# A hybrid Fourier and mLSTM block on one core: the transfers that build block sums issued at other units of the weight stream, and a last block product in fresh banks

## The chip, the cores and the metric

The kernel runs on one core of a Trainium2 chip. The metric is device time in microseconds (us). The kernel before takes 780.82 us (median of 3 runs, 779.57 to 783.08). The profiled execution took 779.69 us, with a span of 777.9 us between its first and its last instruction.

The core's engines run their own instruction streams: TensorE multiplies (PE in the profile; PEld is its weight load), VectorE (DVE), ScalarE (ACT) and GpSimd (POOL) work on tiles, and SyncE (SP) issues transfers. POOL issues some transfers too. Every stream is in order: an instruction that waits holds up what stands behind it.

## The reference

The block has 512 positions (S) and 1024 channels (D), batch 1, one layer:

```python
h = rmsnorm(x, norm_w)
x_f, z_f, x_m, z_m, o_m, g_logits = split(h @ w_in)     # 1024, 1024, 2048, 2048, 2048, 2048 columns
y_a = (fourier_mix(x_f) * silu(z_f)) @ w_fourier        # Re of a 2-D DFT over positions and group channels
x_c = silu(centred_dwconv(x_m))                         # q, k from x_c and v from x_m, block-diagonal
h_cell = mlstm_fwd(q, k, v, gates) + mlstm_bwd(...)     # 4 heads of 512, chunks of 128 positions
h_cell = rmsnorm_per_head(h_cell * sigmoid(o_m)) * hnorm_w
y_b = ((h_cell + skip_w * x_c) * silu(z_m)) @ w_mlstm
g_a, g_b = split(sigmoid(g_logits))
x = x + (g_a * y_a + g_b * y_b) @ w_out
return rmsnorm(x, final_norm_w)
```

All of it is float32.

## The kernel before

**Products.** A float32 product is done as three products of rounded halves: high by high, low by high and high by low (`mm3`, lines 95 to 98). The weights come in units of 128 x 1024 numbers (512 KB), which `plan` lists in their order of use. For each unit SP issues a transfer into one of three buffers `raw` (lines 130 and 133); ScalarE copies the high half (`whi` or `gwh`, `hi_of`, line 86) and VectorE subtracts it for the low half (`wlo` or `gwl`, `lo_of`, line 89). `unit` hands out the next split unit and keeps two items ahead (four once the pool "gw" is open, which is from the stage of the groups on). A transfer can start when the unit that was in its buffer is split.

**Stages.** The units 0 to 16 serve the first projections, 17 to 47 the four heads with their gates, 48 to 63 `w_mlstm`. From unit 64 on come the groups: 16 column groups of `w_in` (the gates of the merge, x_f and z_f) are multiplied by the Strassen-Winograd scheme, seven products of half-size blocks for eight (`group`, with `seventh` and `fourth` for the two products that are put off into the next group). A product there is 12 matmuls of 256 columns, a unit holds two blocks. Between them stands the DFT. Then come eight units of `w_fourier`, then the out-projection by the same scheme in wide form (`wide_product`, seven products on the halves of the 512 rows), the residual, and the final RMSNorm.

**Block sums.** The scheme needs four sums S1 to S4 of blocks of the weights, for four stacks of four groups and for the out-projection (NB = 5 stacks, 20 sums of 1 MB). They are made from DRAM to DRAM: job i (`sum_job`, lines 155 to 162) has SP copy a block into the tile of sum i (line 158), and POOL add another block to sum i-1 with an accumulating transfer (line 162), which has to wait for its copy. In the profile and the program order the tiles are called `sum_76` to `sum_95`: four for each stack, stack 0 (`sum_76` to `sum_79`) being read first, from unit 64 on, and stack 4 (`sum_92` to `sum_95`) by the out-projection. Before, `unit` issues a job each time the next unit to be split is 11, 14, 17 and so on (lines 164 to 168), 21 jobs up to unit 71.

**Heads.** At the end of each head, when its output has been multiplied by the o-gate, the rows are normalised: POOL computes the reciprocal root of four row blocks (`rr`, lines 627 and 628), VectorE scales by it (line 629) and TensorE transposes (line 639). POOL also applies the triangular masks (`wf_...`, AFFINE_SELECT, lines 504 and 507).

**The end.** The out-projection accumulates in X, Z and Y, each two banks of 512 columns, one for each of the two row blocks of 128 (t) in a half of the rows. When a product is done, VectorE adds or subtracts its bank to or from the residual tile `yb` (`add`, line 984). When the last contribution to a tile is in, `part` takes its sum of squares on ScalarE (line 942) and collects it on POOL, and `finish` takes the reciprocal root on POOL (line 953), scales both halves (lines 957, 959, 961) and writes out (line 962). The row blocks 2 and 3 finish before 0 and 1. For row block 1, the last one, the final norm's weight `fn` is multiplied in before (line 949), so that only a scaling by the root is left. The last product is added on top of X, whose bank serves both halves (`0:256`, `256:512`) of row block 1.

**Order.** The program is written in the order of the stages, and a scheduler with a simulated timeline orders the instructions of each engine; `pin` keeps the weight transfers and the copies of the sums in program order on SP. A job moved to another unit therefore also moves what stands around it on SP, POOL and, by way of the weights, on ScalarE.

Of the kernel before, what the change touches and what calls it, by code (L numbers as in the profile page):

```python
# [11 lines left out]
ALU = mybir.AluOpType  # L12
AX = mybir.AxisListType

S = 512
# [4 lines left out]
NRAW = 3  # L20
NG = 16
NB = 5
JOB_AT, JOB_STEP = 11, 3
NWARM = 13
XO = (4, 5, 6, 7, 8, 9, 10, 11, 12, 13, 14, 15, 0, 1, 2, 3)
NU0 = 3
# [13 lines left out]
def hybrid_block(ctx: ExitStack, tc, xT, xn, units, blocks, vecs, gates, gbias, consts, dft, fnw, out):  # L40
    nc = tc.nc
    te, ve, se, gp = nc.tensor, nc.vector, nc.scalar, nc.gpsimd
# [35 lines left out]
    def bank(tag, cols=512, rows=P):  # L78
        count[0] += 1
        return ps.tile([rows, cols], F32, tag=tag, name=f"{tag}_{count[0]}", bufs=4)  # L80
# [41 lines left out]
    state = {"raw": 0, "split": 0, "job": 0}  # L122
# [40 lines left out]

    def unit():
        i = state["split"]
        if i >= JOB_AT and (i - JOB_AT) % JOB_STEP == 0 and state["job"] <= 4 * NB:
            sum_job(state["job"])
            state["job"] += 1
        while len(items) < (4 if "gw" in pools else 2) and state["split"] < nplan:
            prepare()  # L170
        return items.pop(0)
# [63 lines left out]
    def wview(name):  # L235
        return vc[:, name : name + 64].rearrange("p (i d) -> p i d", i=16)
# [18 lines left out]
    ve.tensor_tensor(out=prod, in0=wkr, in1=wview(V_WQ).unsqueeze(2).to_broadcast([P, 16, 4, 4]), op=ALU.mult)  # L255
    ve.tensor_reduce(out=m4, in_=prod, axis=AX.X, op=ALU.add)
    ve.tensor_scalar(out=m4, in0=m4, scalar1=float(512.0 ** -0.5), scalar2=None, op0=ALU.mult)
# [10 lines left out]
    def fold_gates():  # L268
        folded.append(True)
        folds = [tl("sa0", [P, 2, 16, 16]), tl("sb0", [P, 1, 16, 16])]  # L270
        for j, off in enumerate((V_WQ, V_WK, V_WV)):
            dst = folds[j // 2][:, j % 2]
            for half in range(2):
# [3 lines left out]
                ve.tensor_tensor(out=g, in0=g, in1=w, op=ALU.mult)  # L277
                ve.tensor_reduce(out=dst[:, hs, :], in_=g, axis=AX.X, op=ALU.add)
        f = folds[0]
# [83 lines left out]
    for n, (kind, i) in enumerate([("z", 0)] + [("x", i) for i in XO]):  # L363
# [4 lines left out]
        acc = proj(hooks)  # L368
# [76 lines left out]
    half = tl("half", [P, 2, 2])  # L445
# [8 lines left out]
    for h in range(NH):  # L454
# [21 lines left out]
        for d in range(4):  # L476
            acc = bank("wk")
# [70 lines left out]
        for b in range(4):  # L548
            n = (b + 1) * P
# [4 lines left out]
        for acc, first, rest, off in ((sf, 0, (1, 2, 3), P), (sb_, 3, (2, 1, 0), 0)):  # L554
            for b in rest:
                n = (b + 1) * P
                rng = slice(n - P, S) if off else slice(0, n)
                wr = slice(n, 640) if off else slice(0, n)
                if b == rest[0]:
                    full = slice(P, 640) if off else slice(0, S)  # L560
# [31 lines left out]
        for b in range(4):  # L592
            n = (b + 1) * P
# [80 lines left out]
    for q in range(2):  # L674
        accs = [bank("acc") for _ in range(4)]
# [34 lines left out]
    def seventh():  # L710
        X, out1, p5, func, then = prev[0]
        product(X, t_hi, t_lo, 2, False)
        o = out1[:, 256:512]
        ve.scalar_tensor_tensor(out=o, in0=X, scalar=-1.0, in1=p5, op0=ALU.mult, op1=ALU.subtract)
        if func:
            se.activation(o, o, func)

    def fourth():
        X, out1, p5, func, then = prev.pop(0)
        product(X, t_hi, t_lo, 3, False)  # L720
# [4 lines left out]
    def group(out0, out1, func=None, then=None):  # L725
# [4 lines left out]
        if prev:  # L730
            seventh()
        Z = bank("wk")[:, 0:256]
        product(Z, t_hi, t_lo, 0, True)
        se.activation(p5, Z, AF.Copy)
        Y = bank("wk")[:, 0:256]
        product(Y, b_hi, b_lo, 1, True)
        ve.tensor_tensor(out=out0[:, 0:256], in0=Y, in1=p1, op=ALU.add)
        product(X, t_hi, t_lo, 1, False)
        se.activation(u2, X, AF.Copy)
        if prev:  # L740
            fourth()
        product(Z, b_hi, b_lo, 2, False)
        ve.tensor_tensor(out=out0[:, 256:512], in0=Z, in1=u2, op=ALU.add)
        if func:
# [151 lines left out]
    mb, mt = {}, {}  # L896
    for j in range(8):
        ga = gates_a[j]
        wh, wl = unit()
        acc = bank("acc")  # L900
# [16 lines left out]
        else:  # L917
            k = j - 4
# [19 lines left out]
    def part(t, half, cs):  # L938
        y = res[t, half][:, cs]
        sq = t2k()[:, 0 : cs.stop - cs.start]  # L940
        ss = tl("fss", [P, 1], bufs=4)
        se.activation(sq, y, AF.Square, scale=1.0 / 32.0, accum_out=ss)
        if t not in rows:
            rows[t] = tl("rr", [P, 1], bufs=4)
            gp.tensor_scalar(out=rows[t], in0=ss, scalar1=EPS, scalar2=None, op0=ALU.add)
        else:
            gp.tensor_tensor(out=rows[t], in0=rows[t], in1=ss, op=ALU.add)
        if t == 1:
            ve.tensor_tensor(out=y, in0=y, in1=fn[:, half * S + cs.start : half * S + cs.stop], op=ALU.mult)

    def finish(t):
        r = rows[t]
        gp.tensor_tensor(out=r, in0=r, in1=mhalf, op=ALU.pow)
        for half in range(2):
            y = res[t, half]
            if t == 1 and half == 0:
                se.activation(y, y, AF.Copy, scale=r)
            elif t == 1:
                ve.tensor_scalar(out=y, in0=y, scalar1=r, scalar2=None, op0=ALU.mult)
            else:  # L960
                ve.scalar_tensor_tensor(out=y, in0=y, scalar=r, in1=fn[:, half * S : (half + 1) * S], op0=ALU.mult, op1=ALU.mult)
            nc.sync.dma_start(out[t * P : (t + 1) * P, half * S : (half + 1) * S], y)

    full = slice(0, S)

    def wide_product(accs, ms, first, pieces, then):
        ws = [unit() for _ in range(2)]
        for t in range(2):
            ts = slice(t * P, (t + 1) * P)
            for cs in pieces[t]:  # L970
                for k in range(4):
                    wh, wl = (v[:, k % 2 * S + cs.start : k % 2 * S + cs.stop] for v in ws[k // 2])
                    h_, l_ = (v[:, ts] for v in ms[k])
                    acc = accs[t][:, cs]
                    start, stop = first and k == 0, k == 3
                    te.matmul(acc, h_, wh, start=start, stop=False, skip_group_check=True)  # L976
                    te.matmul(acc, h_, wl, start=False, stop=False, skip_group_check=True)  # L977
                    te.matmul(acc, l_, wh, start=False, stop=stop, skip_group_check=True)  # L978
                then(t, cs)

    def add(accs, t0, half, op, last):
        def then(t, cs):
            y = res[t0 + t, half][:, cs]
            ve.tensor_tensor(out=y, in0=y, in1=accs[t][:, cs], op=op)
            if last:
                part(t0 + t, half, cs)
            if last and half == 1 and cs.stop == S:
                finish(t0 + t)
        return then

    whole = [[full], [full]]
    X = [bank("acc") for _ in range(2)]
    Z = [bank("wk") for _ in range(2)]
    Y = [bank("acc") for _ in range(2)]
    blk4 = lambda d, n: [d[n, k] for k in range(4)]
    wide_product(X, blk4(mb, 0), True, whole, add(X, 0, 0, ALU.add, False))
    wide_product(Z, blk4(mt, 0), True, whole, add(Z, 2, 1, ALU.subtract, False))
    wide_product(Y, blk4(mb, 1), True, whole, add(Y, 0, 0, ALU.add, True))
    wide_product(X, blk4(mt, 1), False, whole, add(X, 2, 0, ALU.add, False))
    wide_product(Z, blk4(mb, 2), False, whole, add(Z, 2, 0, ALU.add, True))  # L1000
    wide_product(X, blk4(mt, 2), False, whole, add(X, 2, 1, ALU.subtract, True))
    wide_product(X, blk4(mt, 3), False, [[full], [slice(0, 256), slice(256, S)]], add(X, 0, 1, ALU.subtract, True))

    for key in ("last", "yb", "low", "five", "four", "gw", "high", "edge"):
        close_pool(key)
# [108 lines left out]
```

## Time and profile before

| what | value |
|---|---|
| time, median of 3 (lowest to highest) | 780.82 us (779.57 to 783.08) |
| the profiled execution: time, span | 779.69 us, 777.9 us |
| granted TensorE clock over the span | 0.996 |
| busy: PE, PEld | 761.2 us (98%), 644.8 us (83%) |
| busy: DVE, ACT, POOL | 525.5 us (68%), 409.7 us (53%), 65.1 us (8%) |
| transfers of SP's queue | 106.90 MB, 40.1% of the DMA engines' time |
| transfers of POOL's queue (the accumulates) | 20.97 MB, 14.2% |
| chain that ended last: PE, ACT, DMA, DVE | 93%, 2%, 2%, 1% |

The first two rows are times of whole executions; the span is what the trace covers. The rest comes from the profile of that one execution. An engine's busy share is of the span. The granted clock is the TensorE clock as a share of full speed. The chain is followed back from the last instruction, at each step to what released it.

### The profile page before, as it was taken

Reading aid. Unit: us, or ns where it says so; the run is one execution under the profiler, and the core shown is the slowest. Engines: PE = TensorE matmul, PEld = TensorE weight load, DVE = VectorE, ACT = ScalarE, POOL = GpSimd, SP = SyncE. Lnnn points to the kernel's source line nnn. Section 1 sums busy time; section 2 is a strip of 40 time slices with the busy share of each in tenths; the row PEclk is TensorE's granted clock in tenths of the full one; section 3 lists DMA queues with packets and bytes.
Section 4 is the critical chain, followed back from the end, with each engine's and each line's share of the span. In section 5 each row is a group of like instructions: output and inputs, shape, how many; then the busy total and the mean of one; then the engine's idle time right before and its main releaser. Section 6 shows DMA issues by size and latency. Waiting matters only on the chain.

```text
span 777.9 us, 10932 instructions
## 1 busy us (share of the span) xinstructions
PE 761.2 (98%) x4146; PEld 644.8 (83%) x4146; DVE 525.5 (68%) x811; ACT 409.7 (53%) x640; POOL 65.1 (8%) x139
## 2 busy tenths in 40 slices
PE   9999999999999999999999999988999999999995
PEld 7776676788888888888888888888999999988884
DVE  6599876677758565766585962246767677557875
ACT  7434445659446843785363442255644577643442
POOL 0100000012100300031001000010010100000002
PEclk9999999999999999999999999999999999999999
DMA  8446782065245444246505699798654446554352
GB/s 292 137 163 190 196 236 82 6 184 163 99 118 147 150 134 111 104 112 190 163 28 176 205 300 255 215 264 233 209 171 141 139 156 199 182 176 147 138 190 108
DMA packets 41461, 128.55 MB, mean 165 GB/s; under 512 B 4801, under 2 KB 5314, under 8 KB 36290
## 3 DMA queue, kind: packets, MB, share of 16 engines
q1 hardware_dynamic: 38530, 106.90, 40.1%
q0 software_dynamic: 2880, 20.97, 14.2%
q8 instruction: 32, 0.52, 0.3%
q14 instruction: 19, 0.16, 0.1%
HBM read 125.76 MB, written 44.04 MB: 218 GB/s over the span
## 4 chain that ended last, share of the span: by engine, by line
PE 93%; ACT 2%; DMA 2%; DVE 1%; issue 0%; POOL 0%; SPq 0%; POOLq 0%; ACTq 0%
PE acc L96 17%; PE acc L98 17%; PE acc L97 17%; PE wk L98 7%; PE wk L96 7%; PE wk L97 7%; PE acc L537 3%; PE acc L536 3%; PE acc L538 3%; PE wk L607 2%; PE wk L294 1%; DMA raw<-sum 1%; PE acc L978 1%; PE acc L976 1%; PE acc L977 1%; ACT whi L86 1%
## 5 line engine op out<-in xcount | busy, mean ns | idle before, releaser
L86 ACT ACTIVATE whi<-raw 128x1024 fp32r<-128x1024 f32 (+1 forms) x105 | 108.9, 1039 | 147.5 <-PE acc L97 104.0
L89 DVE TENSOR_TENSOR wlo<-raw,whi 128x1024 fp32r<-128x1024 f32 (+1 forms) x105 | 125.6, 1198 | 84.7 <-ACT whi L86 84.5
L96 PE MATMUL acc<-hhi,whi 128*128 128x512 f32 x248 | 97.3, 396 | 2.0 <-ACT whi L86 2.0
L98 PE MATMUL acc<-hhi,wlo 128*128 128x512 f32 x248 | 97.2, 393 | 0.0
L97 PE MATMUL acc<-hlo,whi 128*128 128x512 f32 x248 | 97.0, 391 | 0.0
L96 PEld LDWEIGHTS acc<-hhi,whi 128*128 128x128 f32 x248 | 46.5, 188 | 15.4 <-ACT whi L86 5.0
L98 PEld LDWEIGHTS acc<-hhi,wlo 128*128 128x128 f32 x248 | 46.6, 188 | 14.6 <-DVE sa L347 2.5
L89 DVE TENSOR_TENSOR gwl<-raw,gwh 128x1024 fp32r<-128x1024 f32 (+1 forms) x39 | 47.1, 1209 | 17.0 <-ACT gwh L86 17.0
L86 ACT ACTIVATE gwh<-raw 128x1024 fp32r<-128x1024 f32 (+1 forms) x39 | 40.8, 1047 | 28.9 <-PE acc L97 9.1
L97 PEld LDWEIGHTS acc<-hlo,whi 128*128 128x128 f32 x248 | 46.6, 188 | 10.1 <-DVE hlo L201 0.9
L538 PE MATMUL acc<-whi,hlo 128*128 128x512 f32 x128 | 50.4, 394 | 0.0
L537 PE MATMUL acc<-wlo,hhi 128*128 128x512 f32 x128 | 50.4, 393 | 0.0
L97 PE MATMUL acc<-sb,whi 128*128 128x512 f32 x128 | 49.9, 391 | 0.0
L96 PE MATMUL acc<-sa,whi 128*128 128x512 f32 x128 | 49.8, 390 | 0.1
L97 PE MATMUL wk<-vlo,phi 128*128 128x512 f32 x128 | 49.8, 389 | 0.0
L96 PE MATMUL wk<-vhi,phi 128*128 128x512 f32 x128 | 49.6, 390 | 0.0
L98 PE MATMUL acc<-sa,wlo 128*128 128x512 f32 x128 | 48.6, 391 | 0.0
L98 PE MATMUL wk<-vhi,plo 128*128 128x512 f32 x128 | 48.0, 389 | 0.0
L536 PE MATMUL acc<-whi,hhi 128*128 128x512 f32 x128 | 47.7, 393 | 0.0
L326 DVE SCALAR_TENSOR_TENSOR t2k<-sa,vecs,t2k 128x511 f32<-128x511 f32 (+1 forms) x64 | 45.7, 747 | 0.4
L96 PEld LDWEIGHTS wk<-vhi,phi 128*128 128x128 f32 x128 | 24.0, 188 | 5.8 <-PE acc L412 0.8
L96 PEld LDWEIGHTS acc<-sa,whi 128*128 128x128 f32 x128 | 24.0, 188 | 5.4 <-ACT whi L86 0.5
(386 smaller groups left out, 1906.2 us busy)
## 6 DMA issues: line engine op xcount, KB each, us to landing
raw<-in_units_dram SPq DMA_DIRECT2D x69, 512.0 KB, 3.8
sum<-in_blocks_dram SPq DMA_DIRECT2D x20, 1024.0 KB, 7.7
raw<-sum SPq DMA_DIRECT2D x64, 256.0 KB, 3.8
raw<-in_blocks_dram SPq DMA_DIRECT2D x48, 256.0 KB, 3.7
sum<-in_blocks_dram POOLq DMA_DIRECT2D x10, 1024.0 KB, 8.5
sum<-sum POOLq DMA_DIRECT2D x10, 1024.0 KB, 8.4
raw<-sum SPq DMA_DIRECT2D x8, 512.0 KB, 4.4
raw<-in_blocks_dram SPq DMA_DIRECT2D x6, 512.0 KB, 4.1
```

Of the source, the lines that this page charges most:

```text
L86: se.activation(dst, src, AF.Copy, scale=scale)
L89: ve.tensor_tensor(out=dst, in0=src, in1=hi.bitcast(F32), op=ALU.subtract)
L96: pin(te.matmul(acc, wh, xh, start=start, stop=False, **skip), pinned)
L97: te.matmul(acc, wh, xl, start=False, stop=False, **skip)
L98: te.matmul(acc, wl, xh, start=False, stop=stop, **skip)
L294: te.matmul(gate_ps[rows, :], w_gate[j][:, i, :], r, start=p < 2, stop=p >= 14, tile_position=(0, 32 * (2 * b + j)))
L326: ve.scalar_tensor_tensor(out=cv[:, o], in0=src[:, s], scalar=cw[k], in1=cv[:, o], op0=ALU.mult, op1=ALU.add)
L536: te.matmul(ops[t], hv(x_hi, k)[:, ts], wh[:, ks], start=k == 0, stop=False)
L537: te.matmul(ops[t], hv(x_hi, k)[:, ts], wl[:, ks], start=False, stop=False)
L538: te.matmul(ops[t], hv(x_lo, k)[:, ts], wh[:, ks], start=False, stop=k == 7)
L607: te.matmul(vp[:, ds], xm[c0 + d][:, b * P : (b + 1) * P], vbf[:, d, :], start=True, stop=True)
L976: te.matmul(acc, h_, wh, start=start, stop=False, skip_group_check=True)
```

## The change

There are four edits. The jobs are issued at a list of units, from 10 to 55 at distances of two and three, instead of every third unit from 11 to 71. The last block product of the out-projection goes into fresh banks, one for row block 0 and one for each half of row block 1, instead of on top of X; since X then lacks it, X is read once more, and subtracted from the first two row blocks' second halves (`both`). The first half of every row block has `fn` multiplied in by VectorE in `part`, and `finish` scales the first half by ScalarE for every row block, not only for row block 1. `banks` and the keys of `accs` only carry these.

```diff
-JOB_AT, JOB_STEP = 11, 3
+JOBS = (10, 12, 14, 16, 18, 20, 23, 25, 28, 30, 33, 35, 37, 39, 41, 44, 46, 49, 51, 53, 55)
...
     def unit():
         i = state["split"]
-        if i >= JOB_AT and (i - JOB_AT) % JOB_STEP == 0 and state["job"] <= 4 * NB:
+        if state["job"] < len(JOBS) and i >= JOBS[state["job"]]:
             sum_job(state["job"])
             state["job"] += 1
...
-        if t == 1:
+        if t == 1 or half == 0:
             ve.tensor_tensor(out=y, in0=y, in1=fn[:, half * S + cs.start : half * S + cs.stop], op=ALU.mult)
...
-            if t == 1 and half == 0:
+            if half == 0:
                 se.activation(y, y, AF.Copy, scale=r)
...
-                    acc = accs[t][:, cs]
+                    acc = accs[t, cs.start][:, cs]
...
-            ve.tensor_tensor(out=y, in0=y, in1=accs[t][:, cs], op=op)
+            ve.tensor_tensor(out=y, in0=y, in1=accs[t, cs.start][:, cs], op=op)
...
-    X = [bank("acc") for _ in range(2)]
-    Z = [bank("wk") for _ in range(2)]
-    Y = [bank("acc") for _ in range(2)]
...
+    def banks(tag):
+        return {(t, 0): bank(tag) for t in range(2)}
+
+    def both(one, two):
+        def then(t, cs):
+            one(t, cs)
+            two(t, cs)
+        return then
...
+    X, Z, Y = banks("acc"), banks("wk"), banks("acc")
...
-    wide_product(X, blk4(mt, 2), False, whole, add(X, 2, 1, ALU.subtract, True))
-    wide_product(X, blk4(mt, 3), False, [[full], [slice(0, 256), slice(256, S)]], add(X, 0, 1, ALU.subtract, True))
+    wide_product(X, blk4(mt, 2), False, whole, both(add(X, 2, 1, ALU.subtract, True), add(X, 0, 1, ALU.subtract, False)))
+    W = {(0, 0): bank("wk"), (1, 0): bank("acc"), (1, 256): bank("acc")}
+    wide_product(W, blk4(mt, 3), True, [[full], [slice(0, 256), slice(256, S)]], add(W, 0, 1, ALU.subtract, True))
```

**The start of the groups.** SP's order before, where the stage of the groups begins (the `raw` loaded from two sources are units of the groups; `dch`, `dpos` and `drow` are the DFT's constants). The last copy, `sum_95`, stands ten rows below `sum_94`, among the same kind of loads.

```order
L158 DMA sum_93<-in_blocks_dram 128x2048
L133 DMA raw_4105<-in_blocks_dram 128x512
L133 DMA raw_4105<-sum_76 128x512
L133 DMA raw_4136<-in_blocks_dram 128x512
L133 DMA raw_4136<-sum_77 128x512
L133 DMA raw_4171<-sum_79 128x512
L133 DMA raw_4171<-in_blocks_dram 128x512
L158 DMA sum_94<-in_blocks_dram 128x2048
L133 DMA raw_4224<-sum_78 128x512
```

SP's order now, around the last two copies; `xr` are the transposed inputs that are read once more while `w_mlstm` is multiplied:

```order
L158 DMA sum_94<-in_blocks_dram 128x2048
L130 DMA raw_3745<-in_units_dram 128x1024
L661 DMA xr_3771<-in_xT_dram 128x512 x2
L130 DMA raw_3791<-in_units_dram 128x1024
L158 DMA sum_95<-in_blocks_dram 128x2048
L130 DMA raw_3823<-in_units_dram 128x1024
L130 DMA raw_3853<-in_units_dram 128x1024
```

The last copies moved out of the groups and stand among the units of `w_mlstm`, nine units' transfers ahead of the first unit of the groups.

ScalarE's order at the same place, before (`gwh` and `whi` are splits of weights, `p`, `u` and `pr` belong to the products, line 745 is the sigmoid):

```order
L86 ACTIVATE gwh_4227<-raw_4171 128x1024
L729 ACTIVATE p_801_4215<-acc_4214 128x256
L734 ACTIVATE p_803_4217<-wk_4254 128x256
L739 ACTIVATE u_802_4216<-acc_4214 128x256
L86 ACTIVATE gwh_4234<-raw_4224 128x1024
L745 ACT_TABLE_LOAD
L745 ACTIVATE pr_4212<-pr_4212 128x512
L729 ACTIVATE p_824_4328<-acc_4327 128x256
L86 ACTIVATE whi_4271<-raw_4231 128x1024
L86 ACTIVATE whi_4304<-raw_4238 128x1024
```

And now:

```order
L86 ACTIVATE gwh_4237<-raw_4227 128x1024
L734 ACTIVATE p_803_4222<-wk_4257 128x256
L739 ACTIVATE u_802_4221<-acc_4219 128x256
L86 ACTIVATE whi_4272<-raw_4234 128x1024
L86 ACTIVATE whi_4305<-raw_4241 128x1024
L729 ACTIVATE p_824_4329<-acc_4328 128x256
L86 ACTIVATE gwh_4345<-raw_4276 128x1024
L745 ACT_TABLE_LOAD
L745 ACTIVATE pr_4217<-pr_4217 128x512
```

Three splits that stood behind the first sigmoid now stand ahead of it.

**POOL in the second head**, before: an accumulate (line 162) stands between the roots of the second and the third row block.

```order
L507 AFFINE_SELECT wf_473_2360<-wf_473_2360 128x128
L627 TENSOR_SCALAR rr_2084<-ss_2067 128x1
L628 TENSOR_TENSOR rr_2084<-rr_2084,mhalf_98 128x1
L627 TENSOR_SCALAR rr_2104<-ss_2067 128x1
L628 TENSOR_TENSOR rr_2104<-rr_2104,mhalf_98 128x1
L162 DMA sum_84<-in_blocks_dram 128x2048
L627 TENSOR_SCALAR rr_2124<-ss_2067 128x1
L628 TENSOR_TENSOR rr_2124<-rr_2124,mhalf_98 128x1
```

And now:

```order
L504 AFFINE_SELECT wf_471_2362<-wf_471_2362 128x128
L162 DMA sum_86<-in_blocks_dram 128x2048
L507 AFFINE_SELECT wf_471_2362<-wf_471_2362 128x128
L504 AFFINE_SELECT wf_472_2363<-wf_472_2363 128x128
L507 AFFINE_SELECT wf_472_2363<-wf_472_2363 128x128
L504 AFFINE_SELECT wf_473_2364<-wf_473_2364 128x128
L507 AFFINE_SELECT wf_473_2364<-wf_473_2364 128x128
L627 TENSOR_SCALAR rr_2088<-ss_2071 128x1
L628 TENSOR_TENSOR rr_2088<-rr_2088,mhalf_98 128x1
L627 TENSOR_SCALAR rr_2108<-ss_2071 128x1
L628 TENSOR_TENSOR rr_2108<-rr_2108,mhalf_98 128x1
L162 DMA sum_87<-sum_85 128x2048
```

The accumulate between the roots is that of another sum, and one more stands ahead of it, among the masks.

**VectorE at the end**, before (line 984 adds a bank, line 961 scales by root and `fn`, line 949 multiplies by `fn`):

```order
L961 SCALAR_TENSOR_TENSOR yb_1243_6870<-yb_1243_6870,rr_7089,sz_1162_6482 128x512
L961 SCALAR_TENSOR_TENSOR yb_1241_6866<-yb_1241_6866,rr_7089,sz_1162_6482 128x512
L984 TENSOR_TENSOR yb_1245_6874<-yb_1245_6874,acc_6877 128x256
L961 SCALAR_TENSOR_TENSOR yb_1238_6860<-yb_1238_6860,rr_6986,sz_1162_6482 128x512
L961 SCALAR_TENSOR_TENSOR yb_1244_6872<-yb_1244_6872,rr_6986,sz_1162_6482 128x512
L949 TENSOR_TENSOR yb_1245_6874<-yb_1245_6874,sz_1162_6482 128x256
L984 TENSOR_TENSOR yb_1245_6874<-yb_1245_6874,acc_6877 128x256
L949 TENSOR_TENSOR yb_1245_6874<-yb_1245_6874,sz_1162_6482 128x256
L959 TENSOR_SCALAR yb_1245_6874<-yb_1245_6874,rr_7004 128x512
```

And now:

```order
L984 TENSOR_TENSOR yb_1245_6874<-yb_1245_6874,acc_6877 128x512
L961 SCALAR_TENSOR_TENSOR yb_1240_6864<-yb_1240_6864,rr_7072,sz_1162_6482 128x512
L961 SCALAR_TENSOR_TENSOR yb_1241_6866<-yb_1241_6866,rr_7091,sz_1162_6482 128x512
L984 TENSOR_TENSOR yb_1244_6872<-yb_1244_6872,wk_7144 128x512
L984 TENSOR_TENSOR yb_1245_6874<-yb_1245_6874,acc_7145 128x256
L949 TENSOR_TENSOR yb_1245_6874<-yb_1245_6874,sz_1162_6482 128x256
L984 TENSOR_TENSOR yb_1245_6874<-yb_1245_6874,acc_7146 128x256
L961 SCALAR_TENSOR_TENSOR yb_1244_6872<-yb_1244_6872,rr_6986,sz_1162_6482 128x512
L949 TENSOR_TENSOR yb_1245_6874<-yb_1245_6874,sz_1162_6482 128x256
```

X is subtracted as a whole further up, the two halves of the last product (`acc_7145`, `acc_7146`) have a bank each, and three of the six scalings of line 961 are gone from VectorE.

More of the change, by code (lines that the diff above doesn't have):

```diff
@@ L991, in hybrid_block, with blk4 @@
     whole = [[full], [full]]
-    X = [bank("acc") for _ in range(2)]
-    Z = [bank("wk") for _ in range(2)]
-    Y = [bank("acc") for _ in range(2)]
-    blk4 = lambda d, n: [d[n, k] for k in range(4)]
+    def banks(tag):
[5 more added lines that the diff above has]
+        return then
+    def blk4(d, n):
+        return [d[n, k] for k in range(4)]
+    X, Z, Y = banks("acc"), banks("wk"), banks("acc")
     wide_product(X, blk4(mb, 0), True, whole, add(X, 0, 0, ALU.add, False))
```

## The prediction

> **What bounds the kernel now.** I read the stretches by engine first, then what TensorE waited for, then the chain of waits, the DMA issues, and last the timeline of the places found. The columns of the first table are the stretch, its length, and the busy time of PE, PEld, DVE, ACT and POOL, then the granted clock, the busy share of the DMA engines and GB/s.
>
> ```profile
> 0.00:504.00 504.00, 500.36 (x2296) 402.21 (x2297) 343.67 (x528) 267.27 (x407) 48.86 (x98) 1.00 0.54 160
> 504.00:536.00 32.00, 27.03 (x203) 25.57 (x202) 13.97 (x17) 15.64 (x24) 2.13 (x5) 0.95 0.96 253
> 536.00:766.00 230.00, 230.00 (x1626) 213.65 (x1625) 162.36 (x256) 123.61 (x202) 11.04 (x29) 1.00 0.51 165
> 766.00:778.00 12.00, 3.85 (x28) 3.33 (x26) 5.55 (x11) 3.19 (x9) 3.11 (x7) 0.85 0.44 166
> ```
>
> TensorE sets the time: 500.36 of the first 504 us and all of 536 to 766. Only two stretches have anything to give: 504 to 536, where the DMA engines are 0.96 busy and TensorE misses 5 us and some clock (0.95), and the last 12 us. What TensorE waited for in the first of them (total, times, longest), and its rows at the second wait, with the slice of 528 to 532:
>
> ```profile
> PE acc L96 <- ACT gwh L86: 2.1, 1, 2.1
> PE wk L96 <- ACT whi L86: 1.8, 1, 1.8
> PE acc L98 <- DVE gwl L89: 0.4, 1, 0.4
> ...
> 525.75 0.28 PE L97 MATMUL wk<-bl,whi 128*128 128x256 f32 x1
> 525.86 0.28 PE L98 MATMUL wk<-bh,wlo 128*128 128x256 f32 x1
> 528.27 0.39 PE L96 MATMUL acc<-bh,gwh 128*128 128x256 f32 x1 [2.12 <-ACT gwh L86]
> ...
> 529.91 0.41 PE L96 MATMUL acc<-bh,gwh 128*128 128x256 f32 x1
> 530.12 0.41 PE L97 MATMUL acc<-bl,gwh 128*128 128x256 f32 x1
> ...
> 528.00:532.00 4.00, 3.31 (x15) 3.01 (x16) 3.50 (x3) 2.11 (x3) 0.00 (x0) 0.59 0.95 197
> ```
>
> Products of 256 columns start every 0.117 us (525.75 to 525.86) and, after the wait, every 0.21 us (529.91 to 530.12): the granted clock was 0.59 from 528 to 532, about 13 products at 0.21. Of the 203 matmuls of the stretch the first 9 have 512 columns and twice that time, so 203 + 9 times 0.117 = 24.8 us of work stand in 32 us: **about 7.3 us are lost here**. Why the weights came late:
>
> ```profile
> 508.62 9.63 DMA raw<-sum
> 518.33 1.06 ACT L86 ACTIVATE whi<-raw 128x1024 fp32r<-128x1024 f32 x1 [2.21 <-DMA raw<-sum]
> ...
> 526.64 0.63 ACT L745 ACTIVATE pr<-pr 128x512 f32<-128x512 f32 x1 [1.25 <-DVE pr L743]
> 527.17 1.99 ACT L86 ACTIVATE gwh<-raw 128x1024 fp32r<-128x1024 f32 x2
> ...
> 498.21 0.50 SPq L158 DMA_DIRECT2D sum<-in_blocks_dram  x1
> 510.87 0.50 SPq L158 DMA_DIRECT2D sum<-in_blocks_dram  x1
> 523.30 0.81 POOL L162 DMA_DIRECT2D sum<-sum  x1 [15.75 <-DMA sum<-in_blocks_dram]
> ```
>
> A weight transfer issued at 508.62 took 9.63 us, and ScalarE started the split at 518.33, as it landed. At that time the last two copies of the block sums (SP, 498.21 and 510.87) and the last accumulates (POOL, 523.30 the last) were under way. The second wait is the same delay at second hand: the sigmoid at 526.64 stands ahead of the weight split at 527.17 in ScalarE's order. From 536 the sums are done, the DMA share is 0.51, and TensorE never waits, with the same products.
>
> **The change, part by part.** (1) *The jobs end at unit 55 instead of 71.* In the new order the last copy is issued between the `w_mlstm` units, where one unit is 5.4 us of TensorE, and nothing but weights and the three small DFT loads is in SP's queue from 486 us on. So all causes of the 7.3 us go; the new order of ScalarE also has three more splits ahead of the first sigmoid. What may remain is the start itself, three raw buffers and a consumption of one unit per 2.8 us (24 products of 0.117). Bounds: nothing remains (536 to 766 shows such products without a wait), or about a third, 2.5 us, if the later wait behind the sigmoid stays (2.1 and 0.4 in the rows above). I take 0.5, nearer the stretch that runs clean: **gain 6.8**.
>
> (2) *Where the jobs go.* The same 20 copies and 20 accumulates are issued at 2 to 3 units' distance from unit 10 on. Cover there is the lead of the weight transfers. The unit issued at 61.66 is split at 75.18; the splits between the two rows belong to units issued before it.
>
> ```profile
> 61.66 0.33 SPq L130 DMA_DIRECT2D raw<-in_units_dram  x1
> 75.18 1.06 ACT L86 ACTIVATE whi<-raw 128x1024 fp32r<-128x1024 f32 x1 [3.31 <-PE acc L97]
> ...
> 54.00:112.00 58.00, 56.61 (x256) 38.69 (x255) 50.57 (x69) 24.11 (x33) 3.55 (x4) 1.00 0.71 200
> 454.00:504.00 50.00, 50.00 (x222) 41.41 (x221) 14.14 (x14) 13.67 (x17) 2.43 (x3) 1.00 0.88 260
> ...
> raw<-in_units_dram SPq DMA_DIRECT2D x10, 512.0 KB, 6.7
> ...
> q0 software_dynamic: 2880, 20.97, 14.2%
> DMA to landing us min/median/max: 5.6/7.7/12.7
> ```
>
> That is 13.5 us of lead. From 454 to 504, with the DMA engines 0.88 busy and a job every 10 to 20 us, weights took 6.7 us (median) and TensorE was busy 50.00 of 50. From 54 to 112 the share is 0.71 now with three copies; five will stand there, and two more jobs are about 2 x 9 us of engine time (an estimate: queue 0's 14.2% of 777.9 us over 20 accumulates, 5.5 us each, and 3.5 for a copy, which moves two thirds as much), which makes about 1.0. The last row is the landing of the 20 copies, least, median and longest. A landing would have to double once more to reach 13.5. I price it at 0, upper bound in the rivals.
>
> (3) *POOL's queue in the second head.* Now POOL's accumulate stands between the reciprocal roots of the second and third row block of head 2, and waits for the copy before it:
>
> ```profile
> 249.40 11.23 SPq L130 DMA_DIRECT2D raw<-in_units_dram  x3
> 260.68 0.50 SPq L158 DMA_DIRECT2D sum<-in_blocks_dram  x1
> ...
> 267.91 0.88 POOL L162 DMA_DIRECT2D sum<-in_blocks_dram  x1 [2.85 <-DMA sum<-in_blocks_dram]
> 268.86 0.18 POOL L627 TENSOR_SCALAR rr<-ss 128x1 f32<-128x1 f32 x1
> ...
> 269.72 0.49 DVE L629 TENSOR_SCALAR so<-so,rr 128x512 f32<-128x512 f32 x1 [1.39 <-POOL rr L628]
> ...
> 269.94 0.49 PE L639 MATMUL wk<-consts,so 128*128 128x128 f32 x3
> ...
> sum<-in_blocks_dram SPq DMA_DIRECT2D x1, 1024.0 KB, 6.8
> sum<-in_blocks_dram POOLq DMA_DIRECT2D x1, 1024.0 KB, 8.7
> ```
>
> The copy lands 6.8 us after issue, POOL goes on at 267.91, the root follows at 268.86, VectorE scales at 269.72 (it waited 1.4), and TensorE's transposes at 269.94 take that row block as it is ready: no slack. The change puts another accumulate (`sum_86`) about 10 us earlier, among POOL's mask instructions; its copy follows the first of the three weights from 249.40 on in SP's order, so it is issued near 249.9 and lands near 257, so it moves data from about 258 to 267 (8.7 us), across the next copy (`sum_87`, same place in SP's order, 260.7). Together they hold about 9 us of engine work from 260.7: the copy lands near 269.5 rather than 267.5, and everything after it, the transposes too, moves. Bounds: 0 (TensorE's other products stand in) and 4 us (accumulate and copy one after the other). I take **1.6 lost**. A wait can also lower the clock, as at 528: 13 products at 0.21 instead of 0.117 are 1.2 us more, which goes to the upper bound.
> [...]
> [...]
>
> (4) *The end.*
>
> ```profile
> 767.88 1.42 DVE L961 SCALAR_TENSOR_TENSOR yb<-yb,rr,sz 128x512 f32<-128x512 f32 x2 [0.42 <-POOL rr L953]
> 769.21 0.41 DVE L984 TENSOR_TENSOR yb<-yb,acc 128x256 f32<-128x256 f32 x1
> 769.68 0.39 PE L976 MATMUL acc<-whi,mdh 128*128 128x256 f32 x1 [1.52 <-DVE yb L984]
> ...
> 773.62 0.72 ACT L957 ACTIVATE yb<-yb,rr 128x512 f32<-128x512 f32 x1 [1.17 <-POOL rr L953]
> 750.34 0.68 DVE L949 TENSOR_TENSOR yb<-yb,sz 128x512 f32<-128x512 f32 x1
> ```
>
> TensorE has done the first half of the last row block at 768.0 and waits until 769.68 for VectorE to read it (769.21), which stood behind two scalings (767.88, 1.42 us); one bank held both halves. Fresh banks take away this 1.68 us. On VectorE the change adds two whole additions and three multiplications of the shape at 750.34 (0.68 each) and takes away three of the six scalings (0.71): 5 x 0.68 - 3 x 0.71 = +1.3 us between 745 and 771. They stand ahead of weight splits and of the reads of the last products. ScalarE gets three scalings (0.72); the one of row block 0 stands ahead of the last square sum, which is on the final chain; most of its 0.72 is waited for: about +0.5. I take 1.68 - 0.5 = **1.1 gained**; bounds 0.3 (the additions also delay a split by 0.8, of their 1.3) and 1.7.
>
> Sum against the profiled execution: 779.69 - 6.8 + 1.6 - 1.1 = 773.4. The median of the three runs is 1.13 above that execution, so I forecast **774.5 us**.
>
> **The rivals.** *Clean* (chance 0.13): no loss in head 2; 774.5 - 1.6 = 772.9, or 772.3 with the whole 1.7 at the end. For it: TensorE lost only 3.6 us in all of the first 504. Against: the transposes have no slack.
> *The group stage keeps half* (0.12): the splits wait for raw buffers and ScalarE's order, not for the sums; 3.5 of 7.3 come back, 774.5 + 3.3 = 777.8. For it: the second wait ended with ScalarE. Against: 536 to 766.
> *Head 2 costs 4 to 6 us* (0.08): copy after accumulate, with a clock dip; 777 to 779.
> *Slower: the early jobs starve the projections* (0.04). SP's queue puts a weight behind each of five copies between 54 and 107. If a copy takes 12.7 us, the longest of the 20, and the weight half its 6.7 after it, the weight lands 16 us after issue against the lead of 13.5. From 13.5 on TensorE waits; five times 2.5 us are 12.5, so 774.5 + 12.5 = 787. Against it: the stretch 454 to 504.
> *It does not do what it says*: the order moved as the list says, so this is no case.
>
> **How the numbers follow.** A change is told from none here at about 0.5%, 3.9 us: faster below 776.9, slower above 784.7. Forecast 0.63, the rivals in their order 0.13, 0.12, 0.08, 0.04. Faster: 0.63 less a few hundredths for its upper edge, plus 0.13, plus a little of the third = 0.77; slower 0.04; the rest 0.19. Low end: 779.7 - 7.3 - 1.7 = 770.7; high end: the half-kept stage, 778.
>
> **What would show it.** Right: from 504 to 536 TensorE busy over 31 us at clock 1.00; no wait of TensorE for VectorE in the last 10 us; the last products about 1.7 us earlier against the end of the stretch before; a new wait of TensorE's transposes (or their weight loads) for VectorE's scaling in head 2, near 270. Wrong: waits for ScalarE remain after 504, the stretch 54 to 112 loses more than its 1.4 us, or VectorE delays a split after 745.

## The result and the profile after

The changed kernel takes 774.93 us (median of 7, 771.72 to 778.67) against 781.93 us for the kernel before (median of 7, 779.57 to 783.08): a ratio of 0.9911, 95% interval 0.9883 to 0.994. It is faster by 7.0 us. The forecast was 774.5 us. The number is close in part by luck: two of the four terms behind it are wrong and one is mis-sized, and the errors cancel.

The profiled execution took 775.75 us (span 774.0). The stretches of the changed kernel, with the columns of the first table of the prediction, and a short one from the middle of them:

```profile
54.00:112.00 58.00, 56.61 (x256) 38.67 (x255) 50.04 (x69) 24.59 (x33) 3.55 (x4) 1.00 0.83 241
...
186.00:454.00 268.00, 264.83 (x1247) 220.39 (x1246) 185.81 (x302) 151.07 (x240) 35.77 (x70) 1.00 0.52 151
454.00:504.00 50.00, 50.00 (x208) 41.18 (x209) 14.97 (x15) 13.35 (x16) 0.82 (x1) 0.94 0.46 140
504.00:536.00 32.00, 32.00 (x245) 30.73 (x244) 17.48 (x21) 19.97 (x31) 0.49 (x3) 1.00 0.65 202
...
454.00:458.00 4.00, 4.00 (x10) 3.13 (x11) 3.09 (x6) 1.83 (x3) 0.82 (x1) 0.50 1.00 400
```

From 504 to 536 TensorE is busy all the time at full clock, as forecast. The projections (54 to 112), where more jobs now stand, lose nothing: 56.61 us busy, to the digit what it was. But a stretch that was clean is no longer clean: just ahead of 454 TensorE stands still, and from 454 to 458 it runs at clock 0.50. That is in the stage of `w_mlstm`. What happened there, in the timeline of the changed kernel (start, duration, instruction, wait before it):

```profile
446.35 0.41 DVE L667 SCALAR_TENSOR_TENSOR xs<-xs,xr 128x256 f32<-128x256 f32 x1
...
446.82 0.80 SPq L661 DMA_DIRECT2D xr<-in_xT_dram  x2
447.67 0.43 SPq L130 DMA_DIRECT2D raw<-in_units_dram  x1
...
452.88 1.06 ACT L86 ACTIVATE whi<-raw 128x1024 fp32r<-128x1024 f32 x1 [2.05 <-DMA raw<-in_units_dram]
...
450.44 0.39 PE L98 MATMUL acc<-sa,wlo 128*128 128x512 f32 x1
453.99 0.79 PE L96 MATMUL acc<-sa,whi 128*128 128x512 f32 x1 [3.17 <-ACT whi L86]
454.58 0.63 PE L97 MATMUL acc<-sb,whi 128*128 128x512 f32 x1
455.01 0.63 PE L96 MATMUL acc<-sa,whi 128*128 128x512 f32 x1
```

And the same transfers in the kernel before:

```profile
439.18 0.43 DVE L667 SCALAR_TENSOR_TENSOR xs<-xs,xr 128x256 f32<-128x256 f32 x1
...
439.67 0.80 SPq L661 DMA_DIRECT2D xr<-in_xT_dram  x2
440.51 0.43 SPq L130 DMA_DIRECT2D raw<-in_units_dram  x1
```

These `xr` rows are the last of four pairs of transfers of the inputs that are read once more (line 661), which share two buffers. SP holds this one back until VectorE has read the buffer (line 667), and a weight transfer stands behind it in SP's order. VectorE has hardly a gap there in either kernel (busy for 15.00 us before and 14.81 now of the 15 from 435 to 450); what differs is its order. The list of units changed what the scheduler put first, and line 667 that frees the buffer now comes at 446.35 instead of 439.18. The weight is issued 7.2 us later, its split starts 5.2 us after that, as it lands (the median landing quoted in the prediction is 6.7), and TensorE waits 3.17 us for its split. Then its matmuls of 512 columns start every 0.43 us instead of 0.23 until 460.

The same points of the program in the two profiled executions give the account: the last transpose of the heads starts at 429.0 instead of 429.7 (the 0.7 arises in the first 10 us), the first product of the groups at 511.27 instead of 505.92, the first product of the out-projection at 728.86 instead of 731.21, and the spans end at 774.0 and 777.9. So the stage of `w_mlstm` lost 6.05 us, the groups gained 7.7, and the end gained 1.55: -0.7 + 6.05 - 7.7 - 1.55 = -3.9.

In the second head, the changed kernel:

```profile
268.95 0.89 POOL L162 DMA_DIRECT2D sum<-sum  x1 [4.57 <-DMA sum<-in_blocks_dram]
...
270.78 0.49 DVE L629 TENSOR_SCALAR so<-so,rr 128x512 f32<-128x512 f32 x1 [3.12 <-POOL rr L628]
...
271.90 0.60 PE L639 MATMUL wk<-consts,so 128*128 128x128 f32 x4
```

And the kernel before:

```profile
272.57 0.60 PE L639 MATMUL wk<-consts,so 128*128 128x128 f32 x4
```

POOL waited 4.57 us instead of 2.85 and VectorE 3.12 instead of 1.39, much as forecast. TensorE lost nothing. The four transposes of this row block are those at 271.90 and, before, at 272.57, not the ones at 269.94 that the prediction took for them: those start 0.2 us into a scaling of 0.49 us, so they cannot read its result. There were 2.4 us of slack, and 0.6 are left.

### The profile page after: what moved, and what is told of

It is laid out like the page before. It is cut to its first block, busy times and chain, and to the rows that moved or that the text cites. A ratio compares the mean times of both kernels' runs of the same rounds, so it can differ in the third digit from the quotient of the medians.

```text
span 774.0 us, 10937 instructions
## 1 busy us (share of the span) xinstructions
PE 760.7 (98%) x4146; PEld 644.8 (83%) x4146; DVE 526.3 (68%) x813; ACT 412.1 (53%) x643; POOL 65.4 (8%) x139
## 4 chain that ended last, share of the span: by engine, by line
PE 92%; DVE 3%; ACT 2%; DMA 1%; issue 1%; POOL 0%; SPq 0%; POOLq 0%; ACTq 0%
PE acc L96 17%; PE acc L98 16%; PE acc L97 16%; PE wk L98 7%; PE wk L96 7%; PE wk L97 7%; PE acc L536 3%; PE acc L537 3%; PE acc L538 3%; PE wk L607 2%; PE wk L294 1%; DMA raw<-in_units_dram 1%; PE acc L978 1%; PE acc L976 1%; PE acc L977 1%; PE wk L639 1%
## 5 line engine op out<-in xcount | busy, mean ns | idle before, releaser
L98 PEld LDWEIGHTS acc<-sa,wlo 128*128 128x128 f32 x128 | 24.7, 193 | 5.4 <-DVE wlo L89 0.3
```

The source lines that it names most:

```text
L98: te.matmul(acc, wl, xh, start=False, stop=stop, **skip)
```

## The experiments

Each run was compared with the kernel before on the same chip; ratios are to it, with 95% intervals.

**The parts apart.** `jobs_only` is the kernel before with the list:

```diff
-JOB_AT, JOB_STEP = 11, 3
+JOBS = (10, 12, 14, 16, 18, 20, 23, 25, 28, 30, 33, 35, 37, 39, 41, 44, 46, 49, 51, 53, 55)
```

> The kernel before with the new list of units alone; the end is as before. Theory (the list brings most of the gain, and takes some of it back by a new wait in the stage of w_mlstm): the stretch 504 to 536 is as full as in the changed kernel (TensorE busy 32 of 32 us, clock 1.00; 7.3 us gained), a wait of about 3.2 us of TensorE for a weight split stands near 451 to 454 with a lower clock behind it (about 6 us lost), and the end costs 1.6 us more than in the changed kernel: 776 to 777 us at the median, ratio to before 0.993. Rival (the end brings most): within 1.5 us of before, ratio 0.998 or more.

776.48 us, ratio 0.9935 (0.9921 to 0.995), as the theory has it; the wait in the stage of `w_mlstm` is there, with 2.7 us. `tail_only` is the changed kernel with the old rule:

```diff
-        if state["job"] < len(JOBS) and i >= JOBS[state["job"]]:
+        if i >= JOB_AT and (i - JOB_AT) % JOB_STEP == 0 and state["job"] <= 4 * NB:
```

> The kernel before with all edits of the end and the old rule for the jobs. Theory: the wait of TensorE for VectorE near 768 (1.5 us) is gone and nothing else moves, so the span falls by 1.6 us: ratio 0.998, 780.3 us against 781.9. Rival (the end brings most of the 7 us): ratio 0.994 or less.

779.8 us, ratio 0.9978 (0.9969 to 0.9987). So the end is worth 1.7 us and the list 5.0. Where, shows in two stretches, first of `jobs_only`:

```profile
446.00:466.00 20.00, 17.27 (x69) 13.47 (x68) 13.52 (x20) 9.21 (x12) 0.82 (x1) 0.91 0.83 249
...
500.00:540.00 40.00, 40.00 (x301) 38.21 (x300) 22.05 (x26) 23.21 (x35) 0.49 (x3) 1.00 0.61 180
```

And of `tail_only`:

```profile
446.00:466.00 20.00, 20.00 (x90) 16.57 (x89) 13.21 (x19) 9.67 (x13) 1.63 (x2) 1.00 0.95 310
500.00:540.00 40.00, 34.49 (x251) 32.50 (x249) 18.73 (x22) 20.47 (x31) 2.14 (x5) 0.96 0.89 249
```

The new loss comes with the list, and the old one goes with it.

**Is it the late jobs?** `late3` puts the last three of the changed kernel's jobs (two copies, three accumulates) back:

```diff
-JOBS = (..., 46, 49, 51, 53, 55)
+JOBS = (..., 46, 49, 65, 68, 71)
```

> The changed kernel with the last three jobs back at their old units 65, 68 and 71. Theory (the late copies and accumulates made the weights late at the start of the groups): TensorE loses about 5 to 7 us again between 500 and 535, waits for splits of 1.5 us and more come back there, with the DMA engines over 0.9 busy. Rival (it was the order of ScalarE, with the sigmoid ahead of a split, or the start of the stage itself, and the changed order cured it): at most 2 us lost there. The wait in the stage of w_mlstm should be smaller or gone where it was the copy ahead of a weight transfer that made it, and stay at about 3 us where the input transfers (line 661) ahead of it in SP's queue make it.

785.12 us, ratio 1.0046 (1.0032 to 1.0061): slower than the kernel before, since it has both losses. Stretches, then what TensorE waited for:

```profile
446.00:466.00 20.00, 15.74 (x62) 12.26 (x61) 13.37 (x22) 8.64 (x11) 0.00 (x0) 0.91 0.46 157
500.00:540.00 40.00, 34.68 (x222) 31.49 (x221) 14.86 (x17) 17.09 (x25) 2.15 (x5) 0.95 0.85 229
```

```profile
PE acc L96 <- ACT whi L86: 4.3, 2, 4.0
PE acc L96 <- ACT gwh L86: 2.1, 1, 2.1
PE wk L96 <- ACT whi L86: 2.1, 1, 2.1
```

The loss at the start of the groups is back, and at some 10 us above the changed kernel it is more than the 5 to 7 expected. The wait near 450 is longest here (4.0), although no job stands near it any more and the DMA engines are only 0.09 busy from 435 to 450 and 0.46 from 446 to 466: the jobs' transfers do not make it.

One rival is left open by this run. With the late jobs ScalarE's order at the start of the groups is the old one again: counted from the first `gwh`, two splits stand ahead of the first sigmoid's table load, as in the kernel before, against five in the changed kernel. The runs on copies and accumulates below tell the two apart.

**The wait for the input transfers.** `xr3` gives these transfers a third buffer:

```diff
-        xr = tl("xr", [P, 2, S], pool="build", bufs=2)
+        xr = tl("xr", [P, 2, S], pool="build", bufs=3)
```

> The changed kernel with three buffers in place of two for the inputs that are read again (xr, line 661), so that the fourth of these transfers waits for the first block_sums and not for the second, and a weight transfer behind it in SP's queue is issued earlier. Theory: the weight is issued some 6 us earlier, the 3.17 us wait near 451 and the low clock behind it (0.50 from 454 to 458) are gone, 6 us of the profiled span: 769 to 771 us at the median, ratio to before 0.985. Rival (the weight was late because the transfers of the sums hold the DMA engines): the weight is issued earlier and lands no earlier, a wait of 2 us or more stays, ratio 0.990 to 0.992 as the changed kernel.

769.95 us (769.61 to 771.09), ratio 0.9852 (0.9836 to 0.9868): the fastest of all, 5 us below the changed kernel. Some of the runs that are set against it below ran on another chip, where the kernel before took 781.46 and 782.06 us instead of 781.51.

SP's timeline (the fourth input transfer and the weight behind it), and the two stretches:

```profile
429.17 0.81 SPq L661 DMA_DIRECT2D xr<-in_xT_dram  x2
435.80 0.33 SPq L130 DMA_DIRECT2D raw<-in_units_dram  x1
```

```profile
446.00:466.00 20.00, 19.98 (x88) 16.22 (x87) 15.37 (x22) 10.63 (x14) 0.27 (x1) 1.00 0.57 158
500.00:540.00 40.00, 40.00 (x317) 38.86 (x316) 24.46 (x30) 24.57 (x38) 0.49 (x3) 1.00 0.68 203
```

Counted through the weight transfers, the one that was issued at 447.67 in the changed kernel is issued at 435.80 here, 11.9 us earlier (some 6 were expected), and both losses are gone. The buffer also changes VectorE's order, so `unit_first` keeps two buffers and moves the weight ahead of the input transfer in SP's queue:

```diff
-            if q == 0 and n < 4:
-                block_sums(n)
...
             wh, wl = unit()
+            if q == 0 and n < 4:
+                block_sums(n)
```

> The changed kernel (two xr buffers) with block_sums called behind the request for the next weights, so that each weight transfer stands ahead of the input transfers (xr) of the same step in SP's queue. Theory (the weight was late because it stood behind an input transfer that waited for its buffer): the wait of 3.17 us and the low clock behind it are gone as with three buffers, 770 to 771 us, ratio 0.985 to 0.987. Rival (VectorE, which was busy without a gap there, delivers too late whatever the order on SP; three buffers helped by letting it work ahead): a wait of 2 us or more stays, ratio 0.990 to 0.992.

772.35 us, ratio 0.9874 (0.9857 to 0.9892). The clock stays at 1.00 there and the longest wait is 1.0 us instead of 3.17. SP's rows, and what is left of TensorE's waits between 446 and 540:

```profile
444.26 0.81 SPq L661 DMA_DIRECT2D xr<-in_xT_dram  x2
445.12 0.43 SPq L130 DMA_DIRECT2D raw<-in_units_dram  x1
```

```profile
PE acc L98 <- DVE wlo L89: 1.0, 1, 1.0
PE acc L96 <- ACT whi L86: 0.5, 1, 0.5
```

The weight now stands behind the third input transfer, which waits for its buffer too (30.5 us, to 444.26); it is issued 2.55 us earlier than in the changed kernel, and that is enough for the long wait to go. The two waits that are left make 1.6 us, and `xr3` has none there; its ratio is lower by 1.7 us, with intervals that just overlap. The longer of the two is a wait for VectorE, which is busy for 16.79 of the 20 us from 446 to 466: the high half is done at 451.06, and the product with the low half starts at 453.33, though such a subtraction takes 1.22 us (median of line 89 in the changed kernel). So the late issue behind an input transfer in SP's queue made the long wait and the low clock, and VectorE's own queue makes a smaller part.

**The late jobs by themselves.** `xr3_late3` is `xr3` with the last three jobs late, as above.

> The kernel with three xr buffers, and the last three jobs at units 65, 68 and 71 again: the loss at the start of the groups without the one in the stage of w_mlstm. Theory (the two losses are independent, and late jobs alone make the first): 7.5 to 8.5 us above xr3, 777.5 to 778.5 us, with waits of TensorE for splits of 2 us and more between 500 and 535 and none near 450. Rival (a delay at one place gives the other more time, so the loss is smaller without the first): 5 us or less above xr3.

780.43 us, ratio 0.9983 (0.9971 to 0.9996): 10.5 us above `xr3`, as `late3` was some 10 above the changed kernel. The two losses are independent; the expected 7.5 to 8.5 us came from profiled executions. From the first product of the groups to one and the same matmul in the last product but one of the out-projection (759.93 in the kernel before) passes 246.3 us in `xr3` and in the changed kernel, and with late jobs 254.0 (the kernel before), 254.7 (`tail_only`), 255.8 (`late3`) and 256.9 us (this): the same lateness costs 7.7 to 10.6 us in four executions. By medians `tail_only` and `xr3`, both with the new end and neither with the loss in `w_mlstm`, stand 9.85 us apart.

Copies or accumulates? `xr3_copies2` adds two copies alone:

```diff
+EXTRA = (65, 68)
+        if i in EXTRA and i not in extra:
+            pin(nc.sync.dma_start(scr[len(extra)], blocks[0, len(extra)], max_dma_last_dim=4 * S * 4))
+            extra.append(i)
```

> The kernel with three xr buffers, and two more copies of 1 MB from DRAM to DRAM into a tile that nothing reads, issued by SP at units 65 and 68, where the last two copies of the sums stood; all jobs stay early, no accumulate is late. It tells the copies from the accumulates. If the copies alone make the weights late: most of the late jobs' loss, 5 us or more above xr3. If it takes the accumulates with them (three of 8 to 9 us each): 0 to 2 us. The work is about two fifths of that of the late jobs in bytes, so in proportion 3 us.

772.94 us, ratio 0.989 (0.9877 to 0.9903): 3.0 us, about the copies' share of the bytes (4 of 13 MB, of 10.5 us; an estimate from the program, which counts a copy's block as read and written and an accumulate's two blocks as read and their sum as written). `xr3_acc3b` holds back the three accumulates alone:

```diff
+        if after is not None:
+            gp.dma_start(sums[b, k][:, 0:16], after[:, 0:16])
         gp.dma_start(sums[b, k], src, accum_op=ALU.add, max_dma_last_dim=4 * S * 4)
...
+        if late and i >= late[0]:
+            late.pop(0)
+            accumulate(20 - len(late), items[-1][0].bitcast(F32))
```

> The kernel with three xr buffers, all copies early, and the last three accumulates held back to the start of the groups: ahead of each, a small transfer of POOL writes 16 columns of the split of a late weight unit into the sum that is accumulated, so that the accumulate waits for that split. (These columns of three sums are therefore wrong, and with them a part of the output.) Two more copies there cost 3.0 us, the late jobs with two copies and three accumulates 10.5 us. Theory (the loss goes with the bytes, read and written: 4 MB for the two copies, 9 MB for the three accumulates): about 7 us above xr3, 776 to 778 us. Rival (the copies and the accumulates are only harmful together, or the copies ahead of the weights in SP's queue are what matters): 3 us or less above xr3.

The small transfer in front makes each of these accumulates wait for the split of a late weight unit; it overwrites 16 columns of the sum, so three sums are not the true ones.

781.51 us, ratio 0.9996 (0.9986 to 1.0005): 11.5 us, more than the late jobs whole. The accumulates, with the small transfers of 8 KB, suffice; the loss is more than their share of the bytes by that estimate (9 of 13 MB, 7.3 of 10.5 us). ScalarE's order is at most a small part of the cause: here four splits stand ahead of the first sigmoid's table load, nearly the new order, while `xr3_copies2` has the two of the old order and loses 3.0 us in all. The median time from issue to landing of the weight halves from 500 to 545 shows the ranking (queue, count, size, us), in `xr3`:

```profile
raw<-sum SPq DMA_DIRECT2D x19, 256.0 KB, 3.7
raw<-in_blocks_dram SPq DMA_DIRECT2D x13, 256.0 KB, 4.2
```

in `xr3_copies2`:

```profile
raw<-sum SPq DMA_DIRECT2D x18, 256.0 KB, 4.4
raw<-in_blocks_dram SPq DMA_DIRECT2D x12, 256.0 KB, 4.5
```

and in `xr3_acc3b`:

```profile
raw<-sum SPq DMA_DIRECT2D x13, 256.0 KB, 5.6
raw<-in_blocks_dram SPq DMA_DIRECT2D x9, 256.0 KB, 8.2
sum<-sum POOLq DMA_DIRECT2D x2, 1024.0 KB, 9.5
```

This run's accumulates do not stand exactly where the late jobs had them, two of them nearly back to back, so its 11.5 us is no measure of the accumulates' part of the 10.5.

**The two halves of the end.** `xr3_noscale` takes the scaling by ScalarE back:

```diff
-        if t == 1 or half == 0:
+        if t == 1:
...
-            if half == 0:
+            if t == 1 and half == 0:
```

> The kernel with three xr buffers, with fresh banks at the end but without the scaling by ScalarE of the first halves of row blocks 0, 2 and 3 (and without the multiplications by the norm's weight ahead of it). Theory of the forecast (the bank is worth 1.7 us, the scaling costs 0.5): 0.5 us faster than xr3 or the same, from the first matmul of the last product but one to the end of the span 16.0 to 16.5 us (16.5 in xr3, 17.95 in the kernel before). Rival (the scaling is part of the gain, since VectorE would else have six scalings ahead of the reads of the last products): 0.5 to 1.5 us slower than xr3.

771.91 us, ratio 0.9877 (0.9865 to 0.989): 2 us slower than `xr3`. `xr3_nobank` keeps that scaling and takes the banks back:

```diff
...
-    W = {(0, 0): bank("wk"), (1, 0): bank("acc"), (1, 256): bank("acc")}
...
+    wide_product(X, blk4(mt, 2), False, whole, add(X, 2, 1, ALU.subtract, True))
+    wide_product(X, blk4(mt, 3), False, [[full], [slice(0, 256), slice(256, S)]], add(X, 0, 1, ALU.subtract, True))
```

> The kernel with three xr buffers and the scaling by ScalarE, but with the last product on top of X as before. Theory of the forecast: the wait of TensorE for VectorE's reading of the first half comes back and the whole is 1 to 1.7 us slower than xr3. Rival (fewer scalings on VectorE let it read the first half earlier, so that the wait goes without the banks): within 0.5 us of xr3.

770.4 us, ratio 0.9859 (0.9846 to 0.9872), not to be told from `xr3`. From the same matmul in the last product but one (the first row of each fence below) to the end of the span pass 17.95 us in the kernel before, 17.9 without the scaling, 16.95 without the banks, and 16.5 with both. In the chain that ended last, of `xr3_noscale`:

```profile
751.91 0.45 PE acc L976 x2
...
761.98 1.41 DVE yb L961 x2
763.40 0.34 DVE yb L984
763.84 0.52 ACT t2k L942 x2
```

and of `xr3`:

```profile
752.88 0.45 PE acc L976 x2
...
759.66 0.59 DVE yb L961
760.33 0.69 DVE yb L984
```

With fresh banks TensorE no longer waits at line 976 (1.5 us in the kernel before, no row in the waits of `xr3_noscale`), but the last addition still stands behind two scalings of VectorE (1.41 us), as it did before. The queue of VectorE was the bound, and TensorE's wait lay beside it. What remains of TensorE's wait with the scaling alone is small:

```profile
PE acc L976 <- DVE yb L984: 0.5, 1, 0.5
```

**How early is too early?** `xr3_dense` issues a job at each unit from 4 to 24.

```diff
+JOBS = tuple(range(4, 25))
```

> The kernel with three xr buffers, and a job at each of the units 4 to 24, all in the projections, to see where an early list starves them. A job is about 9 us of engine time (5.5 and 3.5), and a unit some 1.3 us beside it (0.71 of 58 us less three jobs, over 10.7 units), against 5.4 us of TensorE for a unit. If the DMA engines' time decides: 10.3 us a unit for 20 units, some 4.9 us lost at each, 850 to 870 us in all. If transfers mostly overlap beside each other without loss: under 800 us.

795.38 us in a single run, just under the 800 of the second expectation, but not without loss: it is 25 us above `xr3`. In the projections TensorE starves, with the DMA engines full:

```profile
54.00:112.00 58.00, 43.31 (x180) 30.76 (x178) 38.17 (x54) 15.74 (x22) 4.13 (x5) 0.85 1.02 298
```

The other estimate, 850 to 870 us, took all 20 units to be projections of 5.4 us; the units from 17 on belong to the first head, where they come further apart (in the kernel before 11 splits of weights start from 61.4 to 129.3 us and five from 129.3 to 175.5), and eight of the 21 jobs stand there. The list of the change, one job to two or three units, stays on the safe side of this.

## Why the prediction was right, and where it was not

*The jobs end at unit 55.* Right in place and cause: all of the loss from 504 to 536 went, none of a third of it stayed, and three late jobs bring it back. The term was 6.8 us; it measured 7.7 in the profiled executions and 9.85 between medians. The likely reason for the short size is that the profiled execution of the kernel before was one with little loss there: it took 779.69 us, near the lowest of its seven runs. This is argued from the spread of the runs, not shown. If it is so, adding 1.13 us at the end for the median was an error too, since it takes as lasting what goes with the loss.

*Where the jobs go, priced at 0.* This is the step that failed. Its reason held: the transfers in the projections landed in time, with the DMA engines 0.83 busy there, where the estimate was about 1.0. But it looked at the landings only. The list also moved the order of VectorE in the stage of `w_mlstm`, and with it the release of a buffer that SP waits for, with a weight behind it: 6.05 us in the profiled execution, 4.6 by the ratios of the changed kernel and `xr3` (0.9911 - 0.9852 of 781.9). The order of VectorE could be read without running anything, and SP's waits for line 667 (total, times, longest, from 415 to 462) stand in the profile of the kernel before:

```profile
SPq L661 <- DVE xs L667: 24.5, 2, 15.5
```

*The second head, 1.6 lost.* The mechanism on POOL and VectorE came as told, 1.7 us against the work around it (1.06 us later on the clock, and the work 0.67 earlier). The step "the transposes at 269.94 take that row block as it is ready: no slack" was wrong: 2.4 us of slack took it all.

*The end, 1.1 gained.* Measured 1.55 in the profiled executions and 1.7 by `tail_only`. The sum is near, the split is not: the banks were put at 1.68 gained and the scaling at 0.5 lost, and the profiled executions show the banks alone at 0 and the scaling alone at 1.0.

Between medians the terms are -9.85 (`tail_only` to `xr3`), 4.6 (`xr3` to the changed kernel) and -1.7 (the kernel before to `tail_only`). They lead from the kernel before to the changed one, so that their sum, -6.95, is near the measured -7.0 by construction and is no check of it. The forecast's own sum, -6.8 + 0 + 1.6 - 1.1 = -6.3, was near because what it put too low (3.0 at the groups, 1.6 in the second head, 0.6 at the end) and the 4.6 that it overlooked are of like size, which is luck. None of the rivals had the loss in `w_mlstm`; *Clean* had the second head right. One sum among them is off: of 3.5 us that come back at the groups, 0.5 were in the forecast already, so that rival gives 777.5 us, not 777.8.

## What to carry to other kernels

When a change moves transfers in a program whose order a scheduler makes, read the order of every engine at every queue where a transfer can wait for a buffer, not only at the places where the transfers go: one more buffer (`xr3`) was worth two thirds of what the whole change brought. A wait of TensorE for an engine may lie beside a longer queue on that engine: here removing the wait alone brought nothing (17.9 us to the end against 17.95) until VectorE's queue was shorter (16.5). And the losses that include a lowered clock differed from run to run here (771.72 to 778.67 us in seven runs of the changed kernel, against 769.61 to 771.09 in four of `xr3`, which has neither), so their size is taken from medians, not from one profile.

## What was not expected of the hardware

The same gap of TensorE has different prices. After waits of 2.26 and 0.52 us (`tail_only`, near 520) the granted clock stayed at 1.00; after 2.12 and 0.52 us, 9 us later, it fell. In `xr3_late3` both pairs of waits lowered it, in `late3` it stayed at 1.00 after 2.07 and 0.52 us. In slices of 4 us the falls look unlike (0.80 and 0.58 in the first two rows, of `xr3_late3`), but a slice mixes two clocks. Narrower stretches show 0.50 each time: for 3.4 us in `xr3_late3` (twice), `tail_only` and the kernel before, and for 6.8 us after the 3.17 us of the changed kernel (last row).

```profile
520.00:524.00 4.00, 3.13 (x18) 2.92 (x19) 3.12 (x4) 2.05 (x4) 0.00 (x0) 0.80 0.98 328
...
532.00:536.00 4.00, 4.00 (x21) 4.00 (x22) 2.19 (x2) 0.94 (x2) 0.00 (x0) 0.58 0.69 152
...
532.70:536.10 3.40, 3.40 (x19) 3.40 (x18) 1.51 (x3) 0.38 (x1) 0.00 (x0) 0.50 0.77 176
...
453.10:459.90 6.80, 5.91 (x14) 4.66 (x15) 5.02 (x7) 3.36 (x4) 0.82 (x1) 0.50 0.98 336
```

So the length of a wait alone does not settle its price; what does was not shown. The spread of times goes with it: the seven runs of the changed kernel reach over some 7 us (granted clock 0.997 in the two fastest, 0.991 in the slowest), the four of `xr3`, which has neither loss, over 1.5 us.

One profile shows a clock that cost nothing: that of `xr3_copies2` has 0.947 over the span, and 0.95 from 508 to 516, yet products of 256 columns start there every 0.117 us (67 starts from 508.06 to 515.76), as in `xr3` at 1.00 (512.53 to 518.37), and the execution took 773.66 us against 773.68 in another with 0.998.
